# Probabilities times values: high and low parts summed in PSUM by a third matmul, not by the vector engine

## The chip, the cores and the metric

The kernel runs on one core of one Trainium2 chip. A core has TensorE (PE, with its weight loads listed apart as PEld), VectorE (DVE), ScalarE (ACT), GpSimd (POOL) and SyncE (SP, which issues the DMAs here). The metric is the device time of one execution in microseconds.

## The reference

Two layers of an encoder trunk over 1024 tokens of width 1024. Each layer normalises its input, projects it once, runs three groups of attention heads on it, gates and concatenates their outputs, projects back and adds the normalised result to the residual:

```python
proj = h @ w_in[l]
(dq, dk, dv, dgate, gq, gk, gv, ggate, mq, mgate) = jnp.split(proj, IN_OFFSETS, axis=-1)
# A: 6 heads, two softmaxes each over 1024 keys
p = jax.nn.softmax(s1, axis=-1) - lam * jax.nn.softmax(s2, axis=-1)
oa = jnp.einsum('bhqk,bhke->bhqe', p.astype(v.dtype), v)
# B: 6 query heads on 2 key/value heads, 1024 keys
ob = jnp.einsum('bhgqk,bhkd->bhgqd', softmax(s), v)
# M: 4 heads, 256 memory tokens
om = jnp.einsum('bhsm,bhmd->bhsd', softmax(sm), mv)
y = jnp.concatenate([oa, ob, om], axis=-1) @ w_out[l]
x = x + rms_norm(y, post_norm[l])
```

Each head has 64 value columns. All inputs and outputs are float32.

## The kernel before

Everything is done in float32 accuracy out of cheaper parts. An operand is split into a high part and the rest (`hi`, `lo`), and a product is made of three matmuls, hi·hi, hi·lo and lo·hi. For the attention the split is into two float16 tiles: the probabilities e = exp(...) become `eh` (ACT, line 833, or DVE, line 834) and `el` = e − eh (POOL, line 836, or DVE, line 835); the values lie in `vd`, `vg` and `vm` as rows of 130 columns: 64 of the high part, two of ones (one of which yields the row sum of the softmax), 64 of the low part.

The heads come in items: 12 of group A (`mk_d`, two for each head), 6 of group B (`mk_g`), 4 of group M (`mk_m`) in each layer. An item first finds the maximum of each row of scores (`max_task`, PE lines 1006, 1218/1219, 1275/1276, then a DVE reduction, line 872, `mx`), and puts it with a DMA beside the queries. Then come its units (`stream`, `unit_mm`): PE writes scores for 1024 entries per partition into a two-bank PSUM tile `pp` (lines 1016, 1230/1231, 1286/1287), ACT takes the exponential (line 828), `eh` and `el` follow. After two units (A, B) or one (M), `pv_part` multiplies the probabilities with the values, 128 query rows at a time, so 8 key blocks for each row block in A and B (two row blocks per call) and 2 in M (four row blocks per call). This is `attend`: for each key block one matmul of `eh` with all 130 columns (line 484) and one of `el` with the first 65 (line 485). The high and the low part of the values thus land in different PSUM columns. `pv_part` then copies 65 columns of each row block to the output tile (`od` for A, `og` for B and M) on ACT, line 926, and adds the 64 columns of the low part on DVE, line 927. It does so for two row blocks at a time, 260 columns of one PSUM bank `ps`; for M there are two such rounds. Only one such bank (`"pv"` in `KINDS`) may be held at a time.

Beside the items PE projects: matmuls of line 473 (`matmul_chunk`), whose results are rotated, normalised (DVE, ACT, POOL), transposed (line 640) and stored. When the last item of group A is through, `fin_d` (lines 1107 to 1125) divides and normalises its output on DVE, the result goes to HBM (`y_scr`), comes back as `yt`, and PE transposes it (line 1341). The output projection is line 1371.

The order of the instructions on each engine isn't left to a scheduler. `Plan` is a list scheduler in the kernel itself: it plays every step with a supposed duration (`PE(columns)`, `ACT(n)`, `DVE(n)`), a priority and events, and issues the instructions in the order in which its clock reaches them. `either` gives a step to the engine with the smaller backlog, so `eh`, `el` and the splits of weights (lines 373 and 374) go to DVE, ACT or POOL by the planner's reckoning. On the chip every engine runs its own list strictly in that order, and waits where a semaphore is not there yet. `pv_part` calls for `sum(c for _, c in some) + 200` columns of PE with 206 per key block, for ACT with priority 0 and for DVE with `SV_PRIO` (−1, ahead of others).

## Time and profile before

| what | value |
|---|---|
| median of 3 runs | 1595.51 us (1591.94 to 1596.63) |
| the profiled execution | 1601.95 us |
| its span, first to last instruction | 1600.2 us |
| PE busy | 1497.8 us, 94% |
| PEld busy | 1378.4 us, 86% |
| DVE busy | 1131.6 us, 71% |
| ACT busy | 895.4 us, 56% |
| POOL busy | 847.4 us, 53% |
| mean granted clock of TensorE | 0.974 |

A row of the page that groups instructions gives the line, the engine, the operation, what it writes and reads, the shape, the count, the busy time, the mean of one, and the idle time of the engine before them with what ended it. Matmuls overlap, and so do weight loads: the mean of one is its latency, and the pace is read from the distance of two starts in the timeline. The two layers follow each other, some 800 us each. Within a layer the projections and group A come first (to about 540 us in the first layer and 1320 us in the second), then groups B and M, then the output projection.

### The profile page before, as it was taken

To read this page: it belongs to the slowest core of one execution; us is meant where nothing else is said; L and a number is where in the kernel's file an instruction comes from. 1 tells how busy PE (TensorE), PEld (TensorE's weight loads), DVE (VectorE), ACT (ScalarE), POOL (GpSimd) and SP (SyncE) were. 2 spreads that over 40 slices of the span, in tenths; PEclk is the share of its full clock that TensorE was granted. 3 is DMA by queue.
4 is the path that set the end of the run, shared out by engine and by line. 5 is a ranking of instruction groups with operands and counts; after the bars stand their busy time and mean duration, and the time that the engine had idled before them with its cause. 6 is when DMAs were issued, how large, how long until landed. Compare 5 with 4: busy or idle time off the path is not lost. (4 is left out here: it accounts for less than half of the span.)

```text
span 1600.2 us, 34684 instructions
## 1 busy us (share of the span) xinstructions
PE 1497.8 (94%) x13488; PEld 1378.4 (86%) x13488; DVE 1131.6 (71%) x2241; ACT 895.4 (56%) x1440; POOL 847.4 (53%) x616
## 2 busy tenths in 40 slices
PE   7999999999999778999999999999999996899997
PEld 6998989998999667788889988999889996688886
DVE  7748776888775688865476477778877666889443
ACT  5333757766655665673333356776666556556521
POOL 4234866888645564441132367768876646545300
PEclk9999999999999899999999999999999998899999
DMA  6533322333225244115254423214323334331242
GB/s 203 154 118 111 89 67 84 96 111 89 79 61 141 85 117 108 43 46 188 105 176 120 139 73 98 84 50 115 103 81 93 85 98 129 93 79 46 100 145 92
DMA packets 166030, 163.67 MB, mean 102 GB/s; under 512 B 14853, under 2 KB 140357, under 8 KB 165866
## 3 DMA queue, kind: packets, MB, share of 16 engines
q1 hardware_dynamic: 165866, 161.46, 34.4%
q8 instruction: 106, 1.74, 0.5%
q14 instruction: 58, 0.48, 0.1%
HBM read 110.96 MB, written 50.09 MB: 101 GB/s over the span
## 5 line engine op out<-in xcount | busy, mean ns | idle before, releaser
L836 POOL TENSOR_TENSOR el<-e,eh 128x1024 f16<-128x1024 f32 x266 | 595.1, 2250 | 306.8 <-ACT eh L833 221.6
L473 PE MATMUL ps<-wt,big 128*128 128x256 f32 x3456 | 490.5, 285 | 5.0 <-DVE nat L584 5.0
L872 DVE TENSOR_REDUCE mx<-ps 128x1 f32<-128x512 f32 (+1 forms) x608 | 406.1, 685 | 114.1 <-PE ps L1006 70.1
L473 PEld LDWEIGHTS ps<-wt,big 128*128 128x128 f32 x3456 | 463.7, 191 | 19.8 <-ACT e L828 4.4
L828 ACT ACTIVATE e<-pp 128x1024 f32<-128x1024 f32 x304 | 310.2, 1024 | 144.7 <-PE pp L1016 91.8
L833 ACT ACTIVATE eh<-e 128x1024 f16<-128x1024 f32 x292 | 305.5, 1055 | 2.4
L484 PEld LDWEIGHTS <-eh 128*128 128x128 f16 x2432 | 219.7, 99 | 23.4 <-issue 12.1
L485 PEld LDWEIGHTS <-el 128*128 128x128 f16 x2432 | 219.3, 99 | 8.2 <-DVE el L835 4.3
L374 POOL TENSOR_TENSOR wt<-rt,wt 128x512 fp32r<-128x512 f32 x76 | 106.8, 1416 | 134.3 <-ACT wt L372 103.7
L416 POOL TENSOR_SCALAR u<-ss 128x1 f32<-128x1 f32 (+3 forms) x96 | 24.6, 256 | 260.4 <-DVE ss L1455 120.9
L1006 PE MATMUL ps<-sdk,sdq 96*128 96x512 f32 x384 | 155.5, 413 | 5.1 <-DMA sdk<-s_dkb 2.1
L473 PE MATMUL pp<-wt,big 128*128 128x256 f32 x1152 | 154.6, 289 | 3.2 <-POOL wt L374 1.4
L484 PE MATMUL ps<-vd,eh 128*128 128x130 f16 x1536 | 151.2, 223 | 6.1 <-DVE nat L584 4.4
L473 PEld LDWEIGHTS pp<-wt,big 128*128 128x128 f32 x1152 | 143.4, 193 | 5.8 <-POOL wt L374 1.6
L485 PE MATMUL ps<-vd,el 128*128 128x65 f16 x1536 | 147.8, 194 | 0.0
L1016 PE MATMUL pp<-sdq,sdk 98*128 98x256 f32 x768 | 127.4, 289 | 0.0
L1016 PEld LDWEIGHTS pp<-sdq,sdk 98*128 98x128 f32 x768 | 113.3, 193 | 5.0
L1230 PE MATMUL pp<-big 128*128 128x256 f32 x384 | 103.5, 299 | 0.6 <-ACT e L828 0.5
L1231 PE MATMUL pp<-big 67*128 67x256 f32 x384 | 101.2, 293 | 0.0
L372 ACT ACTIVATE wt<-rt 128x512 fp32r<-128x512 f32 x128 | 78.0, 631 | 24.4 <-DMA rt<-in_w_in 14.3
L1218 PE MATMUL ps<-big 128*128 128x512 f32 x192 | 84.0, 438 | 3.5 <-DMA big<-s_gqb 3.3
L417 POOL TENSOR_TENSOR r<-u,mhalf 128x1 f32<-128x1 f32 (+3 forms) x96 | 80.0, 833 | 8.0
(229 smaller groups left out, 2486.6 us busy)
## 6 DMA issues: line engine op xcount, KB each, us to landing
rt<-in_w_in SPq DMA_DIRECT2D x48, 256.0 KB
rt<-in_w_in SPq DMA_DIRECT2D x96, 128.0 KB
gt<-g_scr SPq DMA_DIRECT2D x32, 256.0 KB
rt<-in_w_out SPq DMA_DIRECT2D x32, 256.0 KB
sdq<-s_dqa SPq DMA_DIRECT2D x48, 128.0 KB
sdk<-s_dka SPq DMA_DIRECT2D x48, 128.0 KB
big<-s_gqa SPq DMA_DIRECT2D x24, 256.0 KB
big<-s_gqb SPq DMA_DIRECT2D x24, 256.0 KB
```

What stands on the lines that cost most here:

```text
L374: (POOL(512, lambda: pool.tensor_sub(out=lo, in0=rt, in1=raw(hi))), W_BIAS[1]))
L473: pe.matmul(ps, lhsT=x[:, kt, :], rhs=y[:, a, :], start=(kt == 0 and n == 0), stop=(kt == KT - 1 and n == 2))
L484: pe.matmul(o[:, 0:130], lhsT=eh, rhs=v[:, kt, 0:130], start=(kt == 0), stop=False, skip_group_check=True)
L485: pe.matmul(o[:, 0:65], lhsT=el, rhs=v[:, kt, 0:65], start=False, stop=(kt == n - 1), skip_group_check=True)
L828: yield ACT(1024, lambda: act.activation(e, ps, AF.Exp, scale=scale), 0, "p")
L833: yield either((ACT(1024, lambda: act.activation(eh, e, AF.Copy)), 0.0), (DVE(1024, lambda: dve.tensor_copy(out=eh, in_=e), 0, fast=True, ...
L836: (POOL(1024, lambda: pool.tensor_sub(out=el, in0=e, in1=eh)), 0.0))
L872: yield DVE(512, lambda: dve.tensor_reduce(out=out_ap, in_=src, axis=AX.X, op=ALU.max), MXP[0])
L1006: yield (512, lambda ps, n=n: pe.matmul(ps, lhsT=q()[0:96, i * P:(i + 1) * P], rhs=k()[0:96, n * 512:(n + 1) * 512], start=True, stop=True ...
L1016: pe.matmul(ps[:, a * 256:(a + 1) * 256], lhsT=k()[0:98, kt * P:(kt + 1) * P], rhs=q()[0:98, j * 256:(j + 1) * 256], start=True, stop=True)
L1230: pe.matmul(o, lhsT=ka()[:, ks], rhs=a()[:, qs], start=True, stop=False)
L1231: pe.matmul(o, lhsT=kb()[0:67, ks], rhs=bb()[0:67, qs], start=False, stop=True)
```

## The change

`attend` now issues three matmuls for each key block: `eh` with the 65 columns of high part and ones, `eh` with the 64 columns of the low part, `el` with 65. All three add up in the same 65 PSUM columns, and the second one's weights, `eh`, are loaded again for it. `pv_part` takes all its row blocks in one round (132 or 264 columns of a bank), and copies them out with one ACT instruction; the DVE addition of line 927 is gone. The planner's numbers move with it: 196 columns for a key block, 100 instead of 200 for a call, ACT's copy at `SV_PRIO`.

```diff
@@ -481,7 +481,8 @@
 
         n = len(es)
         for kt, (eh, el) in enumerate(es):
-            pe.matmul(o[:, 0:130], lhsT=eh, rhs=v[:, kt, 0:130], start=(kt == 0), stop=False, skip_group_check=True)
+            pe.matmul(o[:, 0:65], lhsT=eh, rhs=v[:, kt, 0:65], start=(kt == 0), stop=False, skip_group_check=True)
+            pe.matmul(o[:, 0:64], lhsT=eh, rhs=v[:, kt, 66:130], start=False, stop=False, skip_group_check=True)
             pe.matmul(o[:, 0:65], lhsT=el, rhs=v[:, kt, 0:65], start=False, stop=(kt == n - 1),
                       skip_group_check=True)
 
@@ -912,21 +913,16 @@
             if it.new_o(u):
                 yield from it.alloc_o()
             n = it.n_pv
-            for i0 in range(0, n, 2):
-                slot = yield take_ps("pv")
-                ps = slot[3]
-                some = it.pv_mm(u, ps, tiles, i0)
-                yield PE(sum(c for _, c in some) + 200, lambda: [f() for f, _ in some], PVP)
-                if i0 + 2 >= n:
-                    for b in tiles:
-                        free("e", b[2])
-                    mine.fire(pl)
-                dst = it.o_dst(u)[:, i0:i0 + 2, :]
-                v = ps[:, 0:260].rearrange("p (i d) -> p i d", d=130)
-                yield ACT(130, lambda: act.activation(dst, v[:, :, 0:65], AF.Copy), 0, "p")
-                yield DVE(128, lambda: dve.tensor_add(out=dst[:, :, 0:64], in0=dst[:, :, 0:64], in1=v[:, :, 66:130]),
-                          SV_PRIO)
-                free_ps(slot)
+            slot = yield take_ps("pv")
+            ps = slot[3]
+            some = it.pv_mm(u, ps, tiles, n)
+            yield PE(sum(c for _, c in some) + 100, lambda: [f() for f, _ in some], PVP)
+            for b in tiles:
+                free("e", b[2])
+            mine.fire(pl)
+            v = ps[:, 0:66 * n].rearrange("p (i d) -> p i d", d=66)
+            yield ACT(65 * n, lambda: act.activation(it.o_dst(u), v[:, :, 0:65], AF.Copy), SV_PRIO, "p")
+            free_ps(slot)
             it.pv_done.fire(pl)
 
         def stream(items, kind, t0, du):
@@ -960,17 +956,16 @@
                         boxes, evs = [], []
                 it.free.fire(pl)
 
-        def pv_list(v, ps, tiles, i0, per, stride):
+        def pv_list(v, ps, tiles, n, per, stride):
             out = []
             nk = len(tiles) * per
-            for i in range(i0, i0 + 2):
+            for i in range(n):
                 es = []
                 for kt in range(nk):
                     eh, el, _ = tiles[kt // per]
                     o = (kt % per) * stride + i * P
                     es.append((eh[:, o:o + P], el[:, o:o + P]))
-                c = (i - i0) * 130
-                out.append((lambda c=c, es=es: attend(ps[:, c:c + 130], v, es), 206 * nk))
+                out.append((lambda c=66 * i, es=es: attend(ps[:, c:c + 65], v, es), 196 * nk))
             return out
 
         class Item:
@@ -1019,7 +1014,7 @@
 
             it.loads, it.max_parts, it.unit_mm = loads, max_parts, unit_mm
             it.rows = lambda j: raw(q())[96 + j:97 + j, :]
-            it.pv_mm = lambda u, ps, tiles, i0: pv_list(L.vd[:, h], ps, tiles, i0, 4, 256)
+            it.pv_mm = lambda u, ps, tiles, n: pv_list(L.vd[:, h], ps, tiles, n, 4, 256)
             it.n_pv = 2
             it.new_o = lambda u: u == 1 and m % 2 == 0
 
@@ -1233,7 +1228,7 @@
 
             it.loads, it.max_parts, it.unit_mm = loads, max_parts, unit_mm
             it.rows = lambda j: raw(bb())[65 + j:66 + j, :]
-            it.pv_mm = lambda u, ps, tiles, i0: pv_list(L.vg[:, g // 3], ps, tiles, i0, 4, 256)
+            it.pv_mm = lambda u, ps, tiles, n: pv_list(L.vg[:, g // 3], ps, tiles, n, 4, 256)
             it.n_pv = 2
             it.new_o = lambda u: u == 1
             it.alloc_o = lambda: alloc_og(6 + g)
@@ -1289,7 +1284,7 @@
 
             it.loads, it.max_parts, it.unit_mm = loads, max_parts, unit_mm
             it.rows = lambda j: raw(mb())[65 + j:66 + j, :]
-            it.pv_mm = lambda u, ps, tiles, i0: pv_list(L.vm[:, h], ps, tiles, i0, 2, 512)
+            it.pv_mm = lambda u, ps, tiles, n: pv_list(L.vm[:, h], ps, tiles, n, 2, 512)
             it.n_pv = 4
             it.new_o = lambda u: u == 0
             it.alloc_o = lambda: alloc_og(12 + h)
```

Line numbers after the first hunk of `attend` are one higher in the new kernel, and five lower after `pv_part`. Since the planner's clock runs differently, the order of much else changes. PE has 2432 more matmuls and 2432 more weight loads; DVE has 176 additions less, 18 more of the `el` subtractions (56 for 38), 2 more casts to `eh` (14 for 12) and 6 fewer splits of weights (46 for 52); POOL has 18 fewer `el` (248 for 266) and 6 more splits of weights (82 for 76); ACT has 2 fewer `eh` and 16 fewer copies out (the 32 pairs of M's copies become 16 of four row blocks). SP issues the same 943 DMAs, some of them in another order.

PE at the first product with the values of group M in the first layer (`vm`), before: the last key block of the first two row blocks and what follows.

```order
L484 LDWEIGHTS eh
L484 MATMUL ps_78<-vm,eh 128x130
L485 LDWEIGHTS el
L485 MATMUL ps_78<-vm,el 128x65
L1230 MATMUL pp_75<-big 128x256
L1231 MATMUL pp_75<-big 128x256
```

The same place after; lines 1270 and 1271 are the row maxima of the next item of M (1275 and 1276 before).

```order
L484 LDWEIGHTS eh
L484 MATMUL ps_78<-vm,eh 128x65
L485 LDWEIGHTS eh
L485 MATMUL ps_78<-vm,eh 128x64
L486 LDWEIGHTS el
L486 MATMUL ps_78<-vm,el 128x65
L1270 MATMUL ps_77<-big 128x256
L1271 MATMUL ps_77<-big 128x256
```

A key block is three loads and three matmuls now, and all four row blocks of the unit stand in one stretch of 24 matmuls, where before two stretches of 8 were parted by scores of group B and row maxima.

DVE at the end of group A (the same in both layers), where `fin_d` finishes the last head (`rz`, `ft`) and row maxima (`mx`) of group B stand between its steps, before:

```order
L1107 RECIPROCAL rz<-od 128x16
L1111 SCALAR_TENSOR_TENSOR ft<-od,vc,rz 128x512
L872 TENSOR_REDUCE mx<-ps_79 128x1
L872 TENSOR_REDUCE mx<-ps_80 128x1
L872 TENSOR_REDUCE mx<-ps_77 128x1
L872 TENSOR_REDUCE mx<-ps_78 128x1
L872 TENSOR_REDUCE mx<-ps_79 128x1
L1111 SCALAR_TENSOR_TENSOR ft<-od,vc,rz 128x512
L845 TENSOR_REDUCE nm<-mx 128x8
L1115 TENSOR_TENSOR ft<-ft 128x512
```

The same place after, from the second of the two products of `fin_d` on; between the reciprocal (line 1102 now) and this row stand the first product and two `mx`.

```order
L1106 SCALAR_TENSOR_TENSOR ft<-od,vc,rz 128x512
L873 TENSOR_REDUCE mx<-ps_78 128x1
L873 TENSOR_REDUCE mx<-ps_77 128x1
L873 TENSOR_REDUCE mx<-ps_80 128x1
L873 TENSOR_REDUCE mx<-ps_79 128x1
L873 TENSOR_REDUCE mx<-ps_78 128x1
L873 TENSOR_REDUCE mx<-ps_77 128x1
L873 TENSOR_REDUCE mx<-ps_80 128x1
L873 TENSOR_REDUCE mx<-ps_79 128x1
L873 TENSOR_REDUCE mx<-ps_78 128x1
L1110 TENSOR_TENSOR ft<-ft 128x512
L846 TENSOR_REDUCE nm<-mx 128x8
```

Between the reciprocal and the difference (line 1115 before, 1110 after) five `mx` stood and now eleven do. On PE, 22 score matmuls of 512 columns stand between the last product with `vd` and the transposes of `yt` where 12 stood.

## Rows read from the trace of the kernel before

**Rows 1.** The page's first part, the engines' busy time, and from its second part the granted clock of TensorE in 40 slices of 40 us, in tenths.

```profile
PE 1497.8 (94%) x13488; PEld 1378.4 (86%) x13488; DVE 1131.6 (71%) x2241; ACT 895.4 (56%) x1440; POOL 847.4 (53%) x616
...
PEclk9999999999999899999999999999999998899999
```

**Rows 2.** The view of busy time by stretch, in steps of 100 us: the stretch, its length, busy time of each engine with its count of instructions, then the granted clock, the DMA engines' busy share and GB/s.

```profile
400.00:500.00 100.00, 98.77 (x989) 94.79 (x990) 70.63 (x119) 58.46 (x85) 56.53 (x30) 1.00 0.32 89
500.00:600.00 100.00, 81.70 (x812) 72.25 (x810) 72.50 (x115) 62.26 (x87) 61.14 (x31) 0.93 0.37 104
...
1300.00:1400.00 100.00, 80.21 (x761) 71.03 (x760) 71.97 (x113) 59.91 (x85) 57.14 (x29) 0.88 0.35 98
```

**Rows 3.** The view that groups instructions by line, engine, operation and shape, over the whole span: busy us, mean ns of one, then idle time of the engine before them and what ended most of it.

```profile
L836 POOL TENSOR_TENSOR el<-e,eh 128x1024 f16<-128x1024 f32 x266 | 595.1, 2250 | 306.8 <-ACT eh L833 221.6 <-PE pp L1016 27.1 <-PE ps L473 15.9
...
L485 PEld LDWEIGHTS <-el 128*128 128x128 f16 x2432 | 219.3, 99 | 8.2 <-DVE el L835 4.3 <-issue 3.6
...
L374 POOL TENSOR_TENSOR wt<-rt,wt 128x512 fp32r<-128x512 f32 x76 | 106.8, 1416 | 134.3 <-ACT wt L372 103.7 <-PE pp L473 29.0 <-PE ps L1219 0.9
...
L373 DVE TENSOR_TENSOR wt<-rt,wt 128x512 fp32r<-128x512 f32 x52 | 73.5, 1413 | 9.8 <-ACT wt L372 5.8 <-PE pp L473 2.3 <-POOL wt L374 1.4
...
L835 DVE TENSOR_TENSOR el<-e,eh 128x1024 f16<-128x1024 f32 x38 | 64.6, 1701 | 16.7 <-ACT eh L833 16.5
...
L648 ACT ACTIVATE sh<-ps 128x256 fp32r<-128x256 f32 x84 | 32.1, 383 | 55.8 <-PE ps L640 53.4 <-DMA s_mka<-sl 0.7 <-DVE gm L352 0.5
...
L926 ACT ACTIVATE od<-ps 128x130 f32<-128x130 f32 x96 | 26.9, 280 | 73.3 <-PE ps L485 72.7
L927 DVE TENSOR_TENSOR od<-od,ps 128x128 f32<-128x128 f32 x96 | 26.9, 280 | 19.2 <-ACT od L926 18.9
...
L927 DVE TENSOR_TENSOR og<-og,ps 128x128 f32<-128x128 f32 x80 | 22.4, 280 | 31.6 <-ACT og L926 31.0
...
L834 DVE CAST eh<-e 128x1024 f16<-128x1024 f32 x12 | 11.9, 989 | 2.0 <-ACT e L828 2.0
```

**Rows 4.** The timeline of PE in one call of `pv_part` at full clock: start in us from the span's start, duration, line, tiles, shape. The call has 16 key blocks (32 matmuls); its first four rows, its last, and the matmul that follows it.

```profile
1012.98 0.23 PE L484 MATMUL ps<-vd,eh 128*128 128x130 f16 x1
1013.05 0.19 PE L485 MATMUL ps<-vd,el 128*128 128x65 f16 x1
1013.08 0.22 PE L484 MATMUL ps<-vd,eh 128*128 128x130 f16 x1
1013.14 0.19 PE L485 MATMUL ps<-vd,el 128*128 128x65 f16 x1
...
1014.36 0.19 PE L485 MATMUL ps<-vd,el 128*128 128x65 f16 x1
1014.38 0.48 PE L1006 MATMUL ps<-sdk,sdq 96*128 96x512 f32 x1
```

**Rows 5.** The timeline of PE after a wait inside such a call; in brackets the idle time before and what ended it.

```profile
594.72 0.20 PE L485 MATMUL ps<-vg,el 128*128 128x65 f16 x1 [2.82 <-DVE el L835]
594.76 0.22 PE L484 MATMUL ps<-vg,eh 128*128 128x130 f16 x1
594.82 0.19 PE L485 MATMUL ps<-vg,el 128*128 128x65 f16 x1
```

**Rows 6.** The view of who waited for whom, PE's own: us in total, times, the longest.

```profile
PE ps L1341 <- DMA yt<-y_scr: 17.9, 2, 9.0
...
PE ps L1275 <- DMA big<-s_gqb: 7.3, 4, 2.8
PE ps L848 <- DVE nm L845: 6.0, 4, 1.9
PE ps L473 <- DVE nat L584: 5.0, 4, 2.0
...
PE ps L484 <- DVE nat L584: 4.4, 3, 1.6
PE ps L485 <- DVE el L835: 4.1, 2, 2.8
...
PE ps L484 <- DVE og L927: 1.2, 3, 0.7
...
PE ps L848 <- DVE og L927: 0.7, 1, 0.7
```

**Rows 7.** The timeline of DVE at the end of group A in the second layer.

```profile
1321.94 0.24 DVE L1107 RECIPROCAL rz<-od 128x16 f32<-128x16 f32 x1
1322.22 2.61 DVE L1111 SCALAR_TENSOR_TENSOR ft<-od,vc,rz 128x512 f32<-128x512 f32 x1
1324.76 3.07 DVE L872 TENSOR_REDUCE mx<-ps 128x1 f32<-128x512 f32 x5
...
1328.52 0.69 DVE L1115 TENSOR_TENSOR ft<-ft 128x512 f32<-128x512 f32 x1
```

**Rows 8.** The timeline of PE in between: two score matmuls of 512 columns that follow each other.

```profile
1324.01 0.39 PE L1218 MATMUL ps<-big 128*128 128x512 f32 x1
...
1324.24 0.40 PE L1219 MATMUL ps<-big 65*128 65x512 f32 x1
```

**Rows 9.** The timeline of PE where it takes up the result of that chain.

```profile
1340.70 0.90 PE L1341 MATMUL ps<-ident,yt 128*128 128x128 f32 x3 [9.03 <-DMA yt<-y_scr]
```

## Prediction

> **What bounds the kernel now.** I read the page's busy times first: PE is busy 1497.8 of 1600.2 us, the next engine, DVE, 1131.6 [rows 1]. Busy is a mean, so the stretches of 100 us come next: while group A and the projections run, PE is busy 98.77 of 100 us at full clock; in the stretches with groups B and M it falls to 81.70 and 80.21 at a granted clock of 0.93 and 0.88, with DVE at 72 [rows 2]. So the kernel is bound by PE's own list, and what isn't PE work is mostly a handful of waits in groups B and M. The view of waits names them: the transposes of `yt` wait 17.9 us in two pieces for a round trip through HBM, the operands of M wait for DMAs (7.3 us in the largest row), and the waits that DVE ends are small: `nm` 6.0, `nat` 5.0 and 4.4, `el` 4.1; the addition that goes away is named with 1.2 and 0.7 us [rows 6]. Next, the pace of the matmuls that change. A row gives 0.19 to 0.23 us for one, but that is latency; the distance of starts counts. Sixteen key blocks run from 1012.98 to 1014.38, so one takes 1.40/16 = 87.5 ns. The leg from `el` to the next `eh` (65 columns) is 0.03 us [rows 4], 0.46 us for all sixteen such legs of this call, 28.8 ns each; the leg of 130 columns has the other 58.7.
>
> **The change, part by part.** *The third matmul.* It splits the 130 columns into 65 and 64, and adds 2432 matmuls with 2432 weight loads; the columns go from 195 to 194. Each of the three legs now has 65 columns or 64. The leg of 65 columns that exists already had a fresh weight load in it (its successor's) and took 28.8 ns, so three take 86.4, against 87.5: 1.1 ns less, times 2432 key blocks, 2.7 us less. This is PE's path itself, with nothing beside it. Its cover is that a load fits under a 65-column matmul: what speaks for it is that the load of `eh` does so in all sixteen legs. What no row shows is three such legs in a row, six PE instructions in 87 ns instead of four. The bounds: the slowest start to a next `eh` at full clock is the one behind a wait, 594.72 to 594.76, 40 ns [rows 5]; if the added leg took that, 11.2 ns x 2432 = 27 us more. The other end: legs of 27 ns (the 0.03 of the rows rounded down as far as 65 columns at 2.4 GHz allow) would be 81 ns, 6.5 less, 16 us less. I take −2.7, since it is the value of the same shape in the same burst; −16 and +27 stay for the range.
>
> A weight load of this kind reads 99 ns [rows 3], and yet two of them start in every 87.5 ns [rows 4]: they overlap, so the 99 ns are latency too. A rule speaks against the change here: the Trainium skill, TensorE: Matmul & The Clock Gate, Back-to-back issue gap, puts a stream of pairs of load and matmul at about 81 ns per matmul for 128 columns, both operations setting the pace. By it two pairs took 162 ns and three would take 243, an estimate from that page of 81 x 2432 = 197 us more, a time near 1799 for the profiled execution. The trace disagrees: a pair of 130 columns takes 58.7 ns here and one of 65 columns 28.8 [rows 4], so the sum goes by the trace.
>
> *The addition on DVE* goes: 176 of 280 ns, 49.3 us of DVE work [rows 3]. The planner spends part of it: 18 more `el` at 1.70 us (30.6), 2 casts at 0.99 (2.0), 6 splits fewer at 1.41 (8.5), so DVE has 49.3 − 30.6 − 2.0 + 8.5 = 25.2 us less to do, 2.2% of it. POOL loses 18 x 2.25 = 40.5 and gains 6 x 1.42 = 8.5, 32 us less [rows 3]. All of this lies beside PE's work; the path sees it only in waits. The PSUM bank of the product is held for ACT's copy alone, no longer for copy and addition: the two PE rows that name the addition, 1.2 and 0.7, are gone [rows 6], −1.9 us (0 if PE then waits as long for ACT).
>
> *The copy on ACT* stays as it was for A and B: 280 ns. M's 32 copies of 280 become 16 of 260 columns, near the 383 ns of a 256-column copy [rows 3]: 9.0 − 6.1 = 2.9 us less, on an engine busy 56% [rows 1], so nothing on the path. It goes up in the planner's priorities, so it stands before the `eh` copies it met; what is queued behind a copy that waits for its matmuls is exponentials and `eh`, and behind these the next units.
>
> *The end of group A.* Here the new order has six more `mx` on DVE ahead of the step at line 1115, and 10 more 512-column matmuls on PE ahead of the transposes. In the trace five `mx` take 3.07 us, 0.61 each [rows 7], so `fin_d`'s chain has 6 x 0.61 = 3.7 us more in it, less the addition's 0.28: 3.4. PE has 10 x 0.23 us (the distance of two such starts [rows 8]) = 2.3 us more to do meanwhile. The wait, 9.03 us in the second layer [rows 9], grows by some 1.1 us, in both layers +2.2; the PE work that is moved up isn't lost. Bounds: −4.6 (the chain is as fast as before, and the work moved up fills the wait) to +2.8 (all of the 3.7 is felt).
>
> *Other waits that DVE ends.* `nm`, `nat` twice and `el` are 6.0 + 5.0 + 4.4 + 4.1 = 19.5 us of PE [rows 6]. Less work on DVE and on POOL can shorten them, and a new order can shift them either way; between 0 and −19.5 I take a fifth, −3.5. This is the softest term: a fall of DVE's load by 2.2% alone would give only 0.4, but `el` is the product's last input, and now 18 of them run on the faster of the two engines, 1.70 us for 2.25 [rows 3].
>
> The DMAs are the same 943, and SP's order follows the planner's clock; the loads that groups B and M wait for are still issued when the item before has given its tile free, so I leave these waits (7.3 and the rest) as they are.
>
> The sum: −2.7 − 1.9 + 2.2 − 3.5 = −5.9. The profiled execution took 1601.95 us (span 1600.2 and 1.75 around it); it would take 1596.0. It lies 6.4 us above the median of the three runs, 1595.51, so the forecast for a median is 1589.6, 0.37% less.
>
> **The rivals.** *Nothing moves.* PE stays the bound with the same columns, and the soft terms come out at nothing because another wait takes each one's place: only the third matmul's −2.7 with a part of the rest remains, about 1594. For it: DVE was never on PE's path for more than small waits [rows 6]. Against it: two waits do name the addition.
>
> *The third load isn't covered.* If three short legs in a row can't be fed (the load, or the issue of six instructions in 87 ns), the added leg costs the 40 ns of rows 5: +27 instead of −2.7, so −5.9 + 29.7 = +23.8, about 1619 for a median. It turns the sign from an added leg of 28.8 ns + 5.9 us/2432 = 31.2 ns on. Against it: sixteen of sixteen legs hide a load in 28.8 ns. For it: each of them follows a leg of 58.7 ns, in which the engine could gather ahead. The page named above points the same way, and further.
>
> *The new order meets its waits worse.* PE takes its list in order, ready or not; at the transposes of `yt` or at the operands of M a few microseconds more in each layer give back the gain: if the two rows of DMA waits [rows 6], 25.2 us, grow by a half, +12.6 − 5.9 = +6.7, about 1602.
>
> *DVE was worth more.* If all of the 19.5 us go, −2.7 − 1.9 + 2.2 − 19.5 = −21.9, about 1574; less still if the stretches at 0.93 and 0.88 [rows 2] get a higher clock with it.
>
> That the change doesn't do what it says is excluded: the new list has no addition, and one matmul more for every key block.
>
> **How the numbers follow.** A measurement of this kernel can tell about 0.3%, 4.8 us, from no change, so faster ends at 1590.7 and slower begins at 1600.3. The forecast (1580 to 1593) has 0.34, three quarters of it faster; nothing moves (1593 to 1600) 0.26; the load not covered (1603 to 1640) 0.14; the order meets its waits worse (1600 to 1606) 0.10; DVE worth more (1562 to 1580) 0.16. So faster is 0.26 + 0.16 = 0.42, same 0.08 + 0.26 = 0.34, slower 0.24. The range for 8 in 10 reaches from 1572 to 1612; it leaves out the greater half of the uncovered load and the lower part of the last case. Predicted is the sum, 1589.6.
>
> **What would show it.** In the changed trace a call of 16 key blocks should run in about 48 x 28.8 = 1.38 us, and the legs should be equal; 1.5 us or more means the uncovered load. POOL's `el` should be near 248 x 2.25 = 558 us, DVE near 1106. PE should wait about 10 us at the transposes of `yt` in each layer, and no row should name a copy by ACT in place of the addition with more than 2 us. The prediction is wrong if PE's waits that DVE ends add up to as much as before, or if new waits for `eh`, `el` or DMAs of more than 5 us stand in groups B and M.

## The result and the profile after

The changed kernel takes 1609.57 us, median of 4 runs (1607.88 to 1611.33), beside 1593.72 for the kernel before (1589.76 to 1596.63). The ratio is 1.0101, 95% interval [1.0074, 1.0128]: slower by 1%, where 0.37% faster was forecast. The range (1572 to 1612) holds the time, but only in its upper end. The profiled execution took 1609.8 us, its span is 1608.0, that is 7.8 longer than before's; before's profiled run was one of its longer ones. The kernels of the experiments stood beside 17 to 35 runs of before, with medians from 1596.6 to 1599.1; by those the change costs nearer 0.7%, as two copies of its order (e3 and e4) show. One run of e11, of 5008 us, and one of before beside it, of 7232 us, are left out of all figures.

The page's first part and the granted clock, beside [rows 1]:

```profile
PE 1503.8 (94%) x15920; PEld 1385.6 (86%) x15920; DVE 1094.2 (68%) x2079; ACT 889.3 (55%) x1422; POOL 819.9 (51%) x604
...
PEclk9999999999999888999999999999999998999999
```

DVE is 37.4 us lighter, POOL 27.5, and PE has 2432 matmuls more. None of that is the loss by itself; it says only that the work moved as the diff says. The groups, beside [rows 3], show `el` near the forecast (555.4 for 558) and the copies by ACT at the price supposed (387 ns for the wide ones):

```profile
L837 POOL TENSOR_TENSOR el<-e,eh 128x1024 f16<-128x1024 f32 x248 | 555.4, 2254 | 314.8 <-ACT eh L834 266.8
...
L836 DVE TENSOR_TENSOR el<-e,eh 128x1024 f16<-128x1024 f32 x56 | 82.7, 1484 | 42.0 <-ACT eh L834 40.9
...
L924 ACT ACTIVATE og<-ps 128x260 f32<-128x260 f32 x16 | 6.2, 387 | 11.7 <-PE ps L486 11.4
...
L486 PE MATMUL ps<-vg,el 128*128 128x65 f16 x768 | 82.6, 199 | 13.1 <-POOL el L837 9.6 <-DVE el L836 3.5
```

The last row is the first sign: products of group B stood idle 13.1 us for `el`, three times the 4.1 of before. PE's own waits, beside [rows 6] (us in total, times, longest):

```profile
PE ps L1336 <- DMA yt<-y_scr: 17.4, 2, 10.3
PE ps L486 <- POOL el L837: 9.6, 4, 5.1
PE ps L473 <- DVE nat L585: 8.5, 4, 2.3
PE ps L849 <- DVE nm L846: 8.0, 6, 1.9
...
PE ps L473 <- DVE sl L650: 4.4, 4, 1.8
PE ps L641 <- DVE nat L585: 4.3, 4, 1.9
PE ps L1271 <- DMA big<-s_gqb: 3.7, 4, 1.8
PE ps L486 <- DVE el L836: 3.5, 6, 0.7
```

The two waits for the addition are gone, and so is half of that for `s_gqb`. But `nat` and `nm` grew, and POOL's `el`, which no row of before named, is second. Over the whole view the waits that DVE ends add up to 53.5 us where they were 43.4, those that POOL ends to 11.0 for 2.0, and those for DMAs to 28.6 for 44.6; all named waits together are 95.3 for 92.4.

The pace of the products, beside [rows 4]: the timeline of PE in a call of 16 key blocks, its first four matmuls, its last, and what follows.

```profile
1015.65 0.21 PE L484 MATMUL ps<-vd,eh 128*128 128x65 f16 x1
1015.69 0.20 PE L485 MATMUL ps<-vd,eh 128*128 128x64 f16 x1
1015.73 0.19 PE L486 MATMUL ps<-vd,el 128*128 128x65 f16 x1
1015.76 0.19 PE L484 MATMUL ps<-vd,eh 128*128 128x65 f16 x1
...
1017.09 0.19 PE L486 MATMUL ps<-vd,el 128*128 128x65 f16 x1
1017.12 0.72 PE L473 MATMUL ps<-wt,big 128*128 128x256 f32 x4
```

From 1015.65 to 1017.12 are 1.47 us, 1.463 over 125 such calls (median), against 1.402 before: 91.4 ns for a key block, 3.8 more than before, where 1.1 fewer were forecast. Two legs take 29 ns as supposed; the middle one, from line 485 to 486, is slow in most key blocks (33 to 35 ns).

Last, the longest wait for `el`, in group B of the second layer: ACT, POOL, DVE and PE.

```profile
1384.68 0.63 ACT L372 ACTIVATE wo71h<-rt 128x512 fp32r<-128x512 f32 x1 [2.17 <-DMA rt<-in_w_out]
1386.42 0.63 ACT L372 ACTIVATE wo50h<-rt 128x512 fp32r<-128x512 f32 x1 [1.11 <-DMA rt<-in_w_out]
...
1385.39 3.81 POOL L374 TENSOR_TENSOR wo71l<-rt,wo71h 128x512 fp32r<-128x512 f32 x1 [0.87 <-ACT wo71h L372]
1388.15 7.39 DVE L836 TENSOR_TENSOR el<-e,eh 128x1024 f16<-128x1024 f32 x3
1389.15 2.25 POOL L374 TENSOR_TENSOR wo50l<-rt,wo50h 128x512 fp32r<-128x512 f32 x1
1391.37 3.10 POOL L837 TENSOR_TENSOR el<-e,eh 128x1024 f16<-128x1024 f32 x1
...
1394.52 0.24 PE L486 MATMUL ps<-vg,el 128*128 128x65 f16 x1 [5.07 <-POOL el L837]
```

POOL splits two pieces of `w_out`, whose high parts ACT could make only after waits of 2.17 and 1.11 us for their transfers, and only then makes the `el` that PE's next instruction needs; meanwhile 5.07 us pass on PE. The transfers aren't all of it: the three rows of POOL take 3.81, 2.25 and 3.10 us, where such splits take 1.43 and such an `el` 2.25 on the mean, 4.0 us more in all, and DVE's three `el` beside them 7.39 for 3 x 1.48. Why both are slow here wasn't tried.

### The profile page after: what moved, and what is told of

It is laid out like the page before. It is cut to its first block, busy times and chain, and to the rows that moved or that the text cites. A ratio compares the mean times of both kernels' runs of the same rounds, so it can differ in the third digit from the quotient of the medians.

```text
span 1608.0 us, 39291 instructions
## 1 busy us (share of the span) xinstructions
PE 1503.8 (94%) x15920; PEld 1385.6 (86%) x15920; DVE 1094.2 (68%) x2079; ACT 889.3 (55%) x1422; POOL 819.9 (51%) x604
## 4 chain that ended last, share of the span: by engine, by line
PE 74%; DVE 11%; DMA 6%; issue 4%; POOL 3%; ACT 2%; SPq 1%; POOLq 0%; DVEq 0%; ACTq 0%
PE ps L473 23%; PE pp L473 10%; PE pp L1366 8%; PE ps L1001 5%; PE pp L1011 5%; PE ps L484 4%; DVE mx L873 4%; PE ps L486 4%; PE ps L485 4%; DMA big<-s_gqb 2%; PE pp L1225 2%; PE ps L436 2%; PE pp L1226 2%; PE ps L641 1%; PE ps L1213 1%
## 5 line engine op out<-in xcount | busy, mean ns | idle before, releaser
L837 POOL TENSOR_TENSOR el<-e,eh 128x1024 f16<-128x1024 f32 x248 | 555.4, 2254 | 314.8 <-ACT eh L834 266.8
L873 DVE TENSOR_REDUCE mx<-ps 128x1 f32<-128x512 f32 (+1 forms) x608 | 401.6, 683 | 107.1 <-PE ps L1001 64.9
L484 PEld LDWEIGHTS <-eh 128*128 128x128 f16 x2432 | 227.5, 99 | 17.5 <-issue 10.0
L486 PEld LDWEIGHTS <-el 128*128 128x128 f16 x2432 | 229.3, 101 | 14.3 <-POOL el L837 10.1
L485 PEld LDWEIGHTS <-eh 128*128 128x128 f16 x2432 | 229.6, 99 | 4.3 <-issue 4.1
L374 POOL TENSOR_TENSOR wt<-rt,wt 128x512 fp32r<-128x512 f32 x82 | 116.1, 1428 | 140.1 <-ACT wt L372 95.8
L484 PE MATMUL ps<-vd,eh 128*128 128x65 f16 x1536 | 153.5, 195 | 5.7 <-DVE sl L650 3.3
L485 PE MATMUL ps<-vd,eh 128*128 128x64 f16 x1536 | 152.5, 195 | 0.0
L486 PE MATMUL ps<-vd,el 128*128 128x65 f16 x1536 | 152.0, 193 | 0.0
L416 POOL TENSOR_SCALAR u<-ss 128x1 f32<-128x1 f32 (+3 forms) x96 | 20.9, 218 | 256.5 <-DVE ss L1450 120.9
L836 DVE TENSOR_TENSOR el<-e,eh 128x1024 f16<-128x1024 f32 x56 | 82.7, 1484 | 42.0 <-ACT eh L834 40.9
```

What stands on the lines that cost most here:

```text
L484: pe.matmul(o[:, 0:65], lhsT=eh, rhs=v[:, kt, 0:65], start=(kt == 0), stop=False, skip_group_check=True)
L485: pe.matmul(o[:, 0:64], lhsT=eh, rhs=v[:, kt, 66:130], start=False, stop=False, skip_group_check=True)
L486: pe.matmul(o[:, 0:65], lhsT=el, rhs=v[:, kt, 0:65], start=False, stop=(kt == n - 1), skip_group_check=True)
L837: (POOL(1024, lambda: pool.tensor_sub(out=el, in0=e, in1=eh)), 0.0))
L873: yield DVE(512, lambda: dve.tensor_reduce(out=out_ap, in_=src, axis=AX.X, op=ALU.max), MXP[0])
```

## The experiments

Two theories at first. *Pace*: the third matmul isn't hidden and costs some 4 ns in each of 2432 key blocks. *Order*: the planner's new numbers make a list that meets its waits worse. Below, "planned" is what the planner supposes for a call of 16 key blocks, at the 2346 columns per us of its clock: before 206 x 16 + 200 columns, 1.49 us, for a measured 1.40; after 196 x 16 + 100, 1.38 us, for a measured 1.46. So the change not only made the call longer, it told the planner that it is shorter.

For the accounting of a trace I took the distance of each two starts on PE, subtracted what the same shapes take back to back at full clock, and sorted the excess: over 25 ns is a stall, the rest is pace, and stretches at half clock stand apart. With other values for the back-to-back times the sums of stalls shift by some 30 us and the differences between two kernels by 1 to 3, so only differences are to be read from it; and each kernel has one trace.

### e1: the new products on the old order

```diff
 # before.py, attend: the three matmuls of after.py; pv_part:
-                yield DVE(128, lambda: dve.tensor_add(...), SV_PRIO)
+                yield DVE(128, None, SV_PRIO)     # planned, not issued
```

> The new three matmuls, without the addition, on the old kernel's order: the planner keeps its old numbers and books the addition without issuing it, so every engine's list is that of before, less 176 additions on DVE. Theory P (the pace of three short matmuls): a call of 16 key blocks takes 1.46 us as in the changed kernel, so 9.3 us more than before in all, less up to 1.9 for the addition's waits: 1.005 of before, about 1601. Rival O (the new order): the pace is nothing, the order is all; 0.997 to 1.000 of before.

1600.45 us, ratio 1.0008 [0.9990, 1.0026]. In its trace the same call takes 1.463 us, so the pace is paid in full (6.7 us by the accounting); but stalls fell from 158.8 to 153.6 us and the loss at half clock from 27.1 to 22.7. The second of these is in the main the execution that was profiled: e1's had a mean granted clock of 0.980, its twelve runs have a median of 0.976. Changed products alone: no difference to be measured. So the 9.1 us by which the changed kernel's median lies over e1's must come with the new order (or with the copy's place and M's single round, which e1 leaves as before).

### e2: the old products on the new order

```diff
 # after.py, groups A and B: one matmul of 130 columns, one of 65; behind the copy
+                dve.tensor_add(out=dst[:, :, 0:64], in0=dst[:, :, 0:64], in1=v[:, :, 66:130])   # not planned
```

> The new order with the old products for groups A and B: 130 columns and 65, and the addition on DVE, issued behind ACT's copy without the planner counting it. Group M, 128 of 2432 key blocks, keeps the new form. Theory P: the 16 us lose the pace's 9, 1.004 of before. Rival O: the new order keeps nearly all of the loss, 1.008 to 1.012 of before.

1614.07 us, 1.0106 [1.0084, 1.0128], though pace is back (3.5 us against 3.4 before). The loss stays, as the rival has it. But it isn't a clean undoing, and doesn't show that the order alone holds the loss: the addition is now unplanned, and PE waits for it, `PE ps L1016 <- DVE od L936: 7.3, 16, 0.7` being a new row of its waits; stalls are by the same kind of accounting some 24 us more than in the changed kernel.

### e3, e4, e8: why the middle leg is slow

e3 lets the second matmul read the high part's columns (the low part is left out of the result); e4 keeps the low part in a tile of its own; e8 is e1 with the sequence `eh`·high, `el`·high, `eh`·low.

```diff
 # e3
-            pe.matmul(o[:, 0:64], lhsT=eh, rhs=v[:, kt, 66:130], ...)
+            pe.matmul(o[:, 0:64], lhsT=eh, rhs=v[:, kt, 0:64], ...)
 # e4
-        L.vd = vp.tile([P, 6, NT, 130], F16, name="vd")
+        L.vd = V2(vp.tile([P, 6, NT, 66], F16, name="vd"), vp.tile([P, 6, NT, 64], F16, name="vdl"))
```

> The changed kernel with the middle matmul reading the 64 columns of the high part again in place of the low part, which is left out of the result. Theory A (where the 64 columns begin): in the changed kernel the leg behind the middle matmul is 28 ns where its columns begin at a multiple of 16 bytes (key blocks 3 and 7) and 33 ns elsewhere; here the short legs move to key blocks 0 and 4, and the time stays within 0.3% of the changed kernel's. Rival W (the place of the matmul, behind the same weights and ahead of el): key blocks 3 and 7 stay the short ones.

> The changed kernel with the values' low part in a tile of its own, 64 columns a row, so that each begins at a multiple of 128 bytes; the high part and the ones keep rows of 66 columns. Same order, same count of instructions. Theory A: all middle legs are 28 ns, a call of 16 key blocks takes about 1.40 us and the kernel is 7 to 9 us faster than the changed one, 1.005 of before. Rival W: no change, 1.010 of before.

> The old order with the new products, as in the run with the old order, and the three matmuls of a key block in another sequence: eh with the high part, el with the high part, eh with the low part, so that no weights are loaded twice in a row. Theory W (the slow leg comes from the second load of the same weights or from its place ahead of el): all legs 29 ns, a call takes 1.40 us, 6 us less than with the old order, 0.997 of before. Rival I (a fixed price for each instruction, wherever it lies): 1.46 us as before, 1.001.

e3: 1609.99, 1.0071 [1.0042, 1.0101], a call takes 1.444 us; the middle leg is 28 ns in most key blocks, but the leg behind it is 31 to 32 in half of them. e4: 1609.18, 1.0075 [1.0051, 1.0099], call 1.463; the slow leg has moved to the first (33 to 36 ns). e8: 1604.4, 1.0035 [1.0013, 1.0056], and a call is slower still (14.8 us of pace excess for e1's 10.1). A call of e8 takes 1.495 us. So where the excess falls depends on what is read where, its sum less so (1.44 to 1.50 us for a call), and neither the address of the low part nor a tile of its own removes it.

By key block (medians over the calls with `vd`) the address shows: in the changed kernel the middle leg is 28 ns in key blocks 3 and 7 and 33 to 35 in the others, as theory A says; in e4 it is 28 in six of eight, but the first leg, whose rows of 132 bytes begin at a multiple of 16 only in key blocks 0 and 4, is 33 to 35 ns in the others and 30 and 29 in these two. e3 speaks against it: there the middle leg is 34 ns in key blocks 0 and 4, where A has 28, and 28 elsewhere. Theory A in its simple form, that an aligned low part takes the excess away, has fallen, and theory W with e8; a layout in which all three legs begin at such a multiple wasn't tried, and what the excess is stays open. e3 and e4 also repeat the order of the changed kernel: 1.007 both times.

### e5: the planner told the measured time

```diff
-                out.append((lambda c=66 * i, es=es: attend(ps[:, c:c + 65], v, es), 196 * nk))
+                out.append((lambda c=66 * i, es=es: attend(ps[:, c:c + 65], v, es), 208 * nk))
```

> The changed kernel with one number of the planner's changed: 208 columns for a key block in place of 196, so that a call of 16 key blocks is planned as 1.46 us, what it takes on the chip, in place of 1.38. Nothing of the computation differs, only the order that follows. Theory P2 (the order is worse because the planner thinks the products too short): most of the loss goes, 1.001 to 1.004 of before. Rival E (the loss sits in the steps at the end of group A): in this order no row maxima stand inside the chain of fin_d, so the wait for yt shrinks, but PE has 22 fewer matmuls of 512 columns ahead of it to fill it; 1.003 to 1.006 of before. Rival N (any order other than the old one loses): 1.007 to 1.010.

1590.66 us, 0.9943 [0.9926, 0.9959]: one number, and the changed kernel is faster than both. The pace excess is the same 10.4 us in the trace. At the end of group A no `mx` is left between the reciprocal and the difference in `fin_d` (eleven at 196, five before). Yet the waits are hardly fewer: `PE ps L1336 <- DMA yt<-y_scr: 21.2, 2, 10.6` is longer than the changed kernel's 17.4, and all named waits are 92.2 us for 95.3. What fell is the time at half clock, 49.3 us for 82.6 in the two traces. By the accounting some 15 of the 17.6 us between the two spans are the smaller loss at half clock, and some 3 are stalls. The runs agree: e5's six have mean granted clocks from 0.980 to 0.985, the changed kernel's four from 0.974 to 0.976. The stretches, with the clock third from the end, which is 0.90, 0.95 and 0.90 in the changed kernel:

```profile
500.00:600.00 100.00, 78.97 (x976) 70.90 (x974) 70.02 (x102) 64.58 (x89) 62.60 (x34) 0.91 0.33 93
600.00:700.00 100.00, 94.69 (x1211) 82.67 (x1212) 77.32 (x114) 66.16 (x90) 47.88 (x22) 0.98 0.31 81
...
1300.00:1400.00 100.00, 78.39 (x1050) 69.28 (x1047) 72.14 (x94) 69.47 (x93) 62.33 (x32) 0.93 0.36 99
```

### e6 and e7: which part of the order

e6 plans the addition without issuing it; e7 puts `fin_d` of the last head of group A ahead of other work.

```diff
 # e6, behind the copy
+            yield DVE(64 * n, None, SV_PRIO)
 # e7, fin_d: its steps at priority fp instead of FIN
+            fp = -2 if h == 5 else FIN
```

> The changed kernel with the planner still booking 64 columns per row block on DVE behind ACT's copy, without issuing anything: DVE looks as busy to the planner as before, so it gives el back to POOL (44 on DVE, 260 on POOL, where the changed kernel has 56 and 248). Theory D (the order lost by moving el and casts to DVE): 1.002 of before. Rival N: 1.007 to 1.010. Rival P2: the products are still planned too short, so 1.006 or more.

> The changed kernel with the steps of fin_d for the last head of group A planned ahead of the row maxima (priority -2 in place of 2, for that head alone): 3 of the 11 row maxima stay ahead of the difference, 7 follow behind it. Theory E (the chain at the end of group A is late and with it yt, the loads of w_out and the el behind their splits): 3 to 4 us less in each layer, 1.004 of before, and the wait for yt falls from 10.3 and 7.0 us to 5 or less. Rival N: under 2 us less.

e6: 1604.25, 1.0029 [1.0016, 1.0041]. e7: 1600.14, 1.0007 [0.9987, 1.0028]. Two different repairs: of the 10.5 us by which the changed kernel lies over the 1599.1 of the runs beside them, e7 takes back nearly all and e6 half, e6 mostly at the clock in its trace, which is of one of its faster runs (stalls within 2 us of the changed kernel's, some 9 us less lost at half clock). e7's wait for `yt` has shrunk to 2.1 us, and from the last product of group A to the transposes it is 20.2 us in both layers, as before (20.0 and 20.1; after: 24.4 and 22.6). But the next wait is there already, in PE's waits of e7 and then of e6:

```profile
PE ps L849 <- DVE nm L846: 9.9, 6, 2.6
PE ps L473 <- DVE nat L585: 8.5, 4, 2.3
...
PE ps L486 <- POOL el L837: 7.5, 4, 3.0
```

```profile
PE ps L1337 <- DMA yt<-y_scr: 17.6, 2, 8.8
PE ps L486 <- POOL el L837: 16.7, 15, 2.8
```

### e9 and e10: is a true price a remedy in itself?

```diff
 # e9: before.py
-                out.append((lambda c=c, es=es: attend(ps[:, c:c + 130], v, es), 206 * nk))
+                out.append((lambda c=c, es=es: attend(ps[:, c:c + 130], v, es), 193 * nk))
 # e10: the kernel of e2
-    196 * nk
+    208 * nk
```

> The kernel before with one number changed: 193 columns for a key block where it had 206, so that the planner supposes the measured 1.40 us for a call of 16 key blocks (1.49 before). Products and addition stay. At the end of group A its order keeps five mx between the reciprocal and the difference in fin_d, and twelve 512-column matmuls of PE ahead of the transposes of yt, as before. Theory one (the end of group A carries the time): no change, ratio 0.998 to 1.002. Rival (a true price helps everywhere, by fewer waits in all stages): 0.992 to 0.996, as the re-priced changed kernel had.

> The order of the re-priced changed kernel (208 columns for a key block), but groups A and B with the old products (one matmul of 130 columns, one of 65) and the addition on DVE, which the planner doesn't know of; M keeps three matmuls. Theory one (the third matmul costs 4 ns for a key block even on a good order): PE saves 2304 x 3.8 ns = 8.7 us, the unplanned addition gives back up to half of it, as it did on the order of the changed kernel, so 1582 to 1590, ratio to before 0.990 to 0.995. Rival (the addition, not the third matmul, is the dearer one once DVE's list is planned without it): 1592 to 1600, ratio 0.996 to 1.001.

e9: 1611.58, 1.0073 [1.0051, 1.0095], outside both expectations. With the true price the kernel before becomes slower by as much as the change made it; and the row that the change brought is there, without any change of the products: `PE ps L485 <- POOL el L836: 10.5, 6, 2.8`. e10: 1601.84, 1.0016 [0.9996, 1.0035], just over the rival's band, against e5's 0.9943 on the same order: here the old products with the unplanned addition are dearer, not cheaper, than the three matmuls, and `PE ps L1016 <- DVE od L936: 8.3, 14, 1.0` names the place. My expectation that the third matmul costs its 8.7 us there is wrong.

### e11 to e17: is there a law of the price?

The same line with other numbers: the changed kernel with 202, 214, 220, 232 and 211, the kernel before with 200 and 219.

```diff
-    196 * nk          # e11: 202, e12: 214, e15: 220, e16: 232, e17: 211
-    206 * nk          # kernel before, e13: 200, e14: 219
```

> The changed kernel with 202 columns for a key block, half way between its 196 and the 208 that gave the shorter time. In fin_d's chain at the end of group A six mx stand between reciprocal and difference (eleven at 196, none at 208), and twelve 512-column matmuls of PE ahead of the transposes (22 and none). Theory one (the chain at the end of group A, and with it the splits of w_out and the clock of groups B and M, carries the time): in the middle, 1597 to 1603, ratio 1.000 to 1.004. Rival (each order is a draw of its own, with no dose to it): anywhere from 0.994 to 1.011, and the yt wait and the time not moving together.

> The changed kernel with 214 columns for a key block, above the measured 1.46 us for a call (1.50 supposed). The chain at the end of group A has no mx in it, as with 208. Theory one (the end of group A carries the time): as with 208, 1588 to 1594, ratio 0.993 to 0.997. Rival (the price must meet the measured duration): worse than 208 by as much as 202 is, 1597 to 1603.

> The kernel before with 200 columns for a key block (206 before, 193 in the slower e9): 1.45 us supposed for a call that takes 1.40. At the end of group A no mx stands in fin_d's chain and no 512-column matmul of PE ahead of the transposes (five and twelve at both 193 and 206). Theory one (the longer the supposed price against the measured one, the shorter the time): between 193 and 206, ratio 1.001 to 1.006. Rival (the end of group A carries the time): faster than before, ratio 0.993 to 0.998. Third (each order is a draw): neither, anywhere from 0.990 to 1.010.

> The kernel before with 219 columns for a key block: 1.58 us supposed for a call that takes 1.40. No mx in fin_d's chain. Theory one (a longer supposed price gives a shorter time, whatever the products are): faster than before, ratio 0.988 to 0.996; then the third matmul in itself is worth nothing, and the price all. Rival (the new products are worth 0.8 to 1 per cent at equal price, and the price has done its work at 206): ratio 0.997 to 1.003.

> The changed kernel with 220 columns for a key block: 1.54 us supposed for a measured 1.46. No mx in fin_d's chain, but one el of DVE. Theory one (a longer price gives a shorter time): as 214 or better, 1577 to 1587, ratio 0.987 to 0.993. Rival (a best price close to the measured one, or a draw of the order): above 1590, ratio over 0.995.

> The changed kernel with 232 columns for a key block: 1.63 us supposed for a measured 1.46, 11 per cent too much. Two mx in fin_d's chain and sixteen 512-column matmuls of PE ahead of the transposes. Theory one (a longer price gives a shorter time): 1575 to 1587, ratio 0.986 to 0.993. Rival (past some margin PE's list has too little between the products, so that DVE and ACT get late instead): 1590 to 1600, ratio 0.995 to 1.002.

> The changed kernel with 211 columns for a key block, between 208 (ratio 0.9943) and 214 (0.9895). Nothing of mx in fin_d's chain, as with both neighbours. Theory one (a smooth best place near the measured duration of a call): 0.989 to 0.995, 1580 to 1592. Rival (each number draws an order of its own, of which 214 was the best by chance): outside that, most likely 0.997 to 1.008.

| kernel | columns | planned call, us | median, us | ratio to before, interval |
|---|---|---|---|---|
| before (e9) | 193 | 1.40 | 1611.58 | 1.0073 [1.0051, 1.0095] |
| before (e13) | 200 | 1.45 | 1598.22 | 1.0006 [0.9983, 1.0030] |
| before | 206 | 1.49 | | 1 |
| before (e14) | 219 | 1.58 | 1601.94 | 1.0020 [1.0000, 1.0040] |
| after | 196 | 1.38 | 1609.57 | 1.0101 [1.0074, 1.0128] |
| after (e11) | 202 | 1.42 | 1597.11 | 0.9994 [0.9975, 1.0013] |
| after (e5) | 208 | 1.46 | 1590.66 | 0.9943 [0.9926, 0.9959] |
| after (e17) | 211 | 1.48 | 1589.24 | 0.9941 [0.9920, 0.9962] |
| after (e12) | 214 | 1.50 | 1582.20 | 0.9895 [0.9872, 0.9918] |
| after (e15) | 220 | 1.54 | 1603.30 | 1.0038 [1.0013, 1.0063] |
| after (e16) | 232 | 1.63 | 1601.78 | 1.0031 [1.0009, 1.0053] |

The ratio of the row "after" is to the four runs beside it; to the later runs of before it is near 1.007. e11 and e12 came out under their first theories' bands, e13 in that of the draw alone, e14 and e15 in their rival's, e16 just over its rival's, e17 in that of the smooth curve. The shortest price is the worst for both kernels, and from 196 to 214 the changed one improves step by step (208 and 211 are alike). Then it jumps back: 220, with no `mx` in the chain either, is 1.4% slower than 214. So "the longer, the better" has fallen, and so has "the end of group A alone", for e13 has the chain free and gains nothing: it reaches the transposes 2.7 and 9.0 us sooner after a layer's first product than before did, and its median is the same. What the traces of 214 and 220 show apart is a handful of PE waits of a few us, here 214, then 220:

```profile
PE ps L1336 <- DMA yt<-y_scr: 21.3, 2, 10.6
PE ps L473 <- DVE nat L585: 7.7, 4, 2.0
...
PE ps L486 <- POOL el L837: 5.7, 4, 2.3
PE ps L849 <- DVE nm L846: 4.9, 4, 1.9
```

```profile
PE ps L1336 <- DMA yt<-y_scr: 25.8, 2, 12.9
PE ps L486 <- POOL el L837: 9.8, 6, 3.0
...
PE ps L641 <- DVE nat L585: 7.0, 8, 1.3
PE ps L849 <- DVE nm L846: 6.2, 4, 1.9
PE ps L484 <- DVE mx L873: 4.5, 4, 1.5
PE ps L473 <- DVE nat L585: 4.0, 2, 2.0
```

220 waits 4.5 us more for `yt`, 4.1 for `el`, 1.3 for `nm`, 4.5 for `mx`, and 3.3 for `nat` in two rows instead of one. Each is small; the 17.7 us together are most of the 19.9 between the two spans, and all named waits are 77.5 against 98.2. The accounting agrees: stalls 140.1 against 159.7, clock and pace equal in these two traces. Over all their runs the clock isn't equal, the medians being 0.9825 and 0.9775.

### e18: an order without the wait for yt

With 217 the planner finishes the last product of group A early and puts 54 matmuls of 512 columns and 162 of 256 between it and the transposes (22 and 32 in the changed kernel).

```diff
-    196 * nk
+    217 * nk
```

> The changed kernel with 217 columns for a key block, between 214 (ratio 0.9895) and 220 (1.0038). In its order the last product of group A stands 54 matmuls of 512 columns ahead of the transposes of yt (none at 214 and 220), so the wait for yt should be gone. Theory one (a smooth best place): between its neighbours, 0.990 to 1.003. Theory two (the end of group A carries the time): faster than 214, under 0.990. Rival (a draw): outside, over 1.003, though the yt wait is gone.

1573.1 us, 0.9856 [0.9830, 0.9881]: the fastest of all, and under 0.990, as only theory two had it. The transposes in its second layer, then PE's waits, then two stretches:

```profile
1319.10 0.55 PE L1336 MATMUL ps<-ident,yt 128*128 128x128 f32 x3
```

```profile
PE ps L473 <- DVE nat L585: 12.3, 4, 4.7
PE ps L436 <- DVE xt L456: 7.7, 2, 4.1
PE ps L486 <- DVE el L836: 5.6, 3, 2.7
```

```profile
500.00:600.00 100.00, 90.12 (x1005) 80.08 (x1003) 72.98 (x111) 56.74 (x82) 53.67 (x29) 0.98 0.51 138
...
1300.00:1400.00 100.00, 93.36 (x1093) 82.44 (x1092) 82.05 (x118) 68.70 (x94) 62.01 (x30) 0.95 0.44 123
```

The transposes start without a wait, and neither `yt` nor POOL's `el` is among the waits named. The two stretches that were the weak ones, 81.70 at a clock of 0.93 and 80.21 at 0.88 [rows 2], are now 90.12 at 0.98 and 93.36 at 0.95; the changed kernel had

```profile
500.00:600.00 100.00, 82.26 (x917) 74.38 (x915) 69.50 (x105) 52.78 (x74) 45.66 (x26) 0.90 0.41 114
1300.00:1400.00 100.00, 82.99 (x933) 73.97 (x930) 71.58 (x100) 53.68 (x75) 50.13 (x26) 0.90 0.40 109
```

The time from a layer's first product to these transposes falls by 9.0 and 16.8 us against before (timeline: 379.0 for 388.0, 373.9 for 390.7), in all a little more than the 24.2 by which the span is shorter. But some 8 us of PE's work in each layer, products among it, stand ahead of the transposes in the changed kernel and behind them here. The pace excess is still 10.4 us.

## Why the prediction was wrong

*The bound* was read rightly: PE's list and its waits. *The end of the addition* as well: its waits (1.9 us) went, and no copy by ACT took their place.

*The third matmul* was the first term in error, and against the sum the larger one: −2.7 predicted, +9.3 measured on calls at full clock (3.8 ns x 2432), +6.5 by the accounting of the whole trace. The step that failed is "three legs of the shape that exists take three times 28.8": the rival with the uncovered load named the doubt that each such leg followed a long one. Its turning point, an added leg of 31.2 ns, was passed: 91.4 − 2 x 28.8 = 33.8. Its price (40 ns, 1619 us) was too high, and counts 2.7 us twice, since the 27 us are already what 40 ns cost over 28.8 (1617). What it takes on its own is offset: e1 has the same legs and comes to 1.0008, since the stalls that I had meant to lose went there, −5.2 us for the −1.9 − 3.5 of the sum. On the order of before the size of those terms was right; the reason given for it was so in part only, for e1 leaves the 18 `el` on POOL, and luck has a share.

*The order* was the second error (the terms besides the matmul are 4.1 us off, the matmul 9.2 or 12.0), and the one that makes the changed kernel slower than e1. I kept the gain in stalls as though it came with DVE's lighter load, and looked for what the order costs in one place, the end of group A. On the new order the gain isn't there: stalls 159.7 against 158.8, where the three terms besides the matmul were to give −3.2, and 6.1 more than on the old order with the same products (e1). Another 4.4 us between those two traces are loss at half clock, which is mostly e1's profiled execution and not its kernel.

The step that failed here is the −3.5 for "other waits that DVE ends", together with the DMA waits that were left as they are. The waits for `nm`, `nat` and DVE's `el`, 19.5 us in four rows, came to 24.3 in four, all waits that DVE and POOL end grew by 19.1, and those for DMAs fell by 16.0: the order exchanged one kind of wait for the other. Both signs that the prediction named against itself came true, the waits for DVE not falling and a new wait of more than 5 us for `el` in group B (9.6 in all, behind the splits of `w_out`).

The end of group A itself was nearly as predicted: from the reciprocal to the difference 9.5 us (1329.44 to 1338.98 in DVE's timeline) for 6.6 [rows 7], +3.0 for the 3.4 of the sum, and the named wait didn't grow (17.4 for 17.9). But the time is lost ahead of it: from a layer's first product to the transposes of `yt` the changed kernel takes 395.0 and 396.9 us, e1 389.4 and 388.3, before 388.0 and 390.7, and behind the transposes it isn't slower than before (396.0 for 398.0 us to the next layer's first product, 247.7 for 250.6 to the last matmul). So the late `el` of group B is the most visible new wait, and not what the loss adds up from. The rival "the new order meets its waits worse" was right in kind, with 0.10; it looked at `yt` and the operands of M, where the waits fell, and not at DVE's and POOL's rows, where they rose.

*What I did not ask at all*: whether the planner's new number was true. 196 columns a key block and 100 a call mean 1.38 us, just what I forecast myself (48 x 28.8), where the call takes 1.46; before, a plan of 1.49 stood over 1.40. The plan went from 6% too long to 6% too short. e5, e18 and the table show that this number moves the time by 2.3% (1609.57 to 1573.10 us) with the products untouched, more than anything the products do. That the loss goes with the number is shown, since only it differs between the changed kernel and e5. It doesn't act in one way: e5, e6 and e11 have the stalls of the changed kernel and less loss at half clock, e12 and e18 have some 20 us of stalls less besides. That a true or a longer number is better is not a law: 220 and 232 lose again, and 193 in the kernel before was true and slow.

Are the new products worth anything? Over the prices tried, those of the table and 217, the kernel before ranges from 1.0000 to 1.0073, the changed one from 0.9856 to 1.0101; on one order, old or new, e1 says 1.0008 and e5 against e10 0.7% for the three matmuls, e10 with its addition unplanned. With the order left out, between nothing and a small gain, which is the size forecast, but orders differ by more than that. Why an order meets fewer waits than another was followed only at the places named, and the copy's new priority and M's single round weren't tried apart.

## What to carry to other kernels

When a change alters both an operation and the numbers by which a static order is planned, compare the planned duration with the one in the trace, and try the old products on the new order and the new ones on the old before judging the operation. On engines that run a fixed list, a saving on an engine that isn't the bound is only worth the waits that go in that very list; look for a piece of work to put into the longest remaining wait (here some 35 us of scores and projections ahead of `yt`) before shaving instructions. Planner numbers as near as 217 and 220 can be 1.8% apart, so sweep several and don't read a law out of three.

## What the runs showed of the hardware

Three matmuls of 65, 64 and 65 columns with a fresh load each take 91.4 ns at full clock, 30.5 a leg, against 27.1 for the columns. In the same kernel at half clock the third matmul adds nothing: a key block takes 164 ns there (median of 156), as it does in the kernel before (median of 110). The stretch 1384.30 to 1386.80 has a granted clock of 0.50 there, in the view by stretch, and the timeline of PE reads

```profile
1384.33 0.25 PE L484 MATMUL ps<-vg,eh 128*128 128x65 f16 x1
1384.38 0.24 PE L485 MATMUL ps<-vg,eh 128*128 128x64 f16 x1
1384.44 0.24 PE L486 MATMUL ps<-vg,el 128*128 128x65 f16 x1
1384.49 0.24 PE L484 MATMUL ps<-vg,eh 128*128 128x65 f16 x1
```

0.16 us for three legs, near the 162 ns of 194 columns at 1.2 GHz. So the excess at full clock isn't a share of the columns' time; whether it is there at half clock too, hidden under the longer columns, these rows don't tell. The Trainium skill, TensorE: Matmul & The Clock Gate, Back-to-back issue gap, has about 81 ns for each pair of load and matmul at 128 columns; neither kernel comes near it, since three such pairs of half the columns take 91.4 ns here and one of 130 took 58.7 [rows 4]. The time at half clock differs between kernels of the same work: 83.7 us before, 82.6 after, 49.3 in e5, 53.6 in e18, and what sets it wasn't tried. It differs between runs of one kernel as well: 121 runs of the kernel before have mean granted clocks from 0.970 to 0.984 and times from 1608.0 down to 1588.2 us, 1603.9 in the median where the clock is 0.974 or less and 1593.2 where it is 0.980 or more. So one trace against one trace can mistake the clock of an execution for a gain of the kernel.
